# Split halves of the conv outputs' pair sums: adding DMAs or VectorE

## The chip, the cores and the metric

The kernel runs on one core of a Trainium2 chip. The metric is the device time of one launch in microseconds. TensorE (PE) multiplies, VectorE (DVE), ScalarE (ACT) and GpSimd (POOL) work element by element, SyncE (SP) issues DMAs, and GpSimd and ScalarE issue some too. Each engine takes its instructions strictly in the order in which they stand in its own list; an instruction that waits for a semaphore holds up all that stand behind it on that engine.

## The reference

One layer of an encoder on 512 tokens of width 1024, in float32. The attention part (a softmax branch and a stick-breaking branch, gates, an output projection) takes the first half of the run and is not touched here. What matters is the feed-forward part:

```python
def conv_glu(x, w_up, conv_w, conv_b, w_down):
    hid = x @ w_up
    hid = lax.conv_general_dilated(
        hid, conv_w[:, None, :], window_strides=(1,),
        padding=((CONV_WIDTH - 1, 0),),
        dimension_numbers=('NWC', 'WIO', 'NWC'),
        feature_group_count=2 * D_FF) + conv_b
    gate, up = hid[..., :D_FF], hid[..., D_FF:]
    return (jax.nn.silu(gate) * up) @ w_down
```

with `D_FF` = 2816, a convolution of width 3 along the tokens, and x + conv_glu(norm(x)) as the output.

## The kernel before

**Precision.** A float32 product is made of three faster ones: each operand is split into a rounded part (`hi`, a cast on ScalarE) and the rest (`lo`, a subtraction on VectorE), and TensorE adds hi·hi, hi·lo and lo·hi.

**The up-projection** (chunks `up0` to `up21`, 128 gate and 128 up features each). For chunk j TensorE makes the two products against the transposed tokens (`hth`, `htl`), either plainly (`up_body`, 48 matmuls of 512 columns) or, for the twelve chunks in `SEVEN`, by Strassen's scheme in seven products of half the size (`up_seven`, 84 matmuls of 256 columns), whose weight combinations lie in DRAM (`parked`) and are loaded as `wxh`/`wxl` and `w2h`/`w2l`. `conv` then makes the convolution: an activation on ScalarE (L990) and two operations on VectorE (L992, L993), for the gate into `cg` and for the up part into `ub`, a buffer of four slots of 512 tokens, one per chunk. SiLU (L1014) and a product (L1089) make the chunk's output in `ub`. While chunk j is multiplied, the weights of chunk j+1 are split: ScalarE casts `raw_up` into `whi_up` (L242, L271), VectorE subtracts for `wlo_up` (L243, L276), and SP loads the weights after that.

**The pairs.** The down-projection is made by Strassen's scheme too, over pairs of chunks: pair i is chunks 2i and 2i+1, and its seven left operands, each split in two, are kept in `ax` (2048 wide: four operands' hi, then their lo) and `ay` (1536 wide: three operands). They come out of `ub` in two ways: some are its own halves of 256 tokens or their difference in place (`u`, the convolution's output: 768 wide for `ax`, 256 for `ay`), the others are sums that VectorE makes at L1044 into `st` (256 wide for `ax`, 512 for `ay`). `st` is one buffer for all pairs; nothing of the next pair can be written to it until all that read it are done.

`up_fin` calls `pair_sums` behind each odd chunk. For pairs 1 to 8 the split is made by `by_dma`. ScalarE writes the rounded and negated source into the place of the lo half (L1061), a DMA that GpSimd issues adds the source onto it (L1062), and ScalarE casts the source into the place of the hi half (L1063):

```python
A.activation(a[:, n + o:n + sl.stop], src, AF.Copy, scale=-1.0)
G.dma_start(a[:, n + o:n + sl.stop].bitcast(F32), src, accum_op=ALU.add)
A.copy(a[:, sl], src)
```

This is done four times in a pair, for `ay<-st`, `ax<-st`, `ay<-ub` and `ax<-ub`. The other pairs (0, 9 and 10) use `halves`: a cast on ScalarE (L1052) and a subtraction on VectorE (L1053).

**Keeping them.** For pairs 0 to 6 GpSimd then writes `ay` to DRAM (`ayd`, L1095), since there are two buffers for it; SP writes `ax` of pairs 0 and 1 to DRAM (`axd`, L1097). They are loaded again before the down-projection (L1126, L1236).

**The down-projection** (`dn`, L1269) multiplies all pairs' operands with the down weights, in two passes.

**The order.** The kernel's text gives the instructions, and a scheduler with its own estimate of times sets the order on each engine; a change in one place so moves others by a few positions. GpSimd's DMAs need room in SBUF for their descriptors, which is set when the program is made (`dynamic_dma_scratch_size`).

Of the kernel before, what the change touches and what calls it, by code (L numbers as in the profile page):

```python
# [8 lines left out]
F32 = mybir.dt.float32  # L9
# [6 lines left out]
P = 128  # L16
# [58 lines left out]
def block_kernel(ctx: ExitStack, tc: tile.TileContext, x, xt, params, g2, rbx, wts, wd0, wd1, out):  # L75
    nc = tc.nc
    V, A, G, PE, SP = nc.vector, nc.scalar, nc.gpsimd, nc.tensor, nc.sync
# [4 lines left out]
    sm = ctx.enter_context(tc.tile_pool(name="sm", bufs=1))  # L82
# [5 lines left out]
    def apool(name):  # L88
        return ap_ctx.enter_context(tc.tile_pool(name=name, bufs=1))
# [2 lines left out]
        apool(n) for n in ("pv", "pst", "pqn", "ppt", "pwk", "po")]  # L92
    pool_c = apool("pc")
    pool_pk = apool("ppk")
    par = sm.tile([P, 280], F32, tag="par", name="par")
    A.dma_start(par[:, 0:8], params[:, 0:8])
    A.preload_act_table_set("exp_and_others")
    WARM = 9
# [190 lines left out]
    def run_chunk(key, body, pieces=4):  # L289

        sp = split_gen(pos[key] + 1, pieces)
        for _ in body(*splits.pop(key)):
            next(sp, None)
            yield
        for _ in sp:
            pass
# [17 lines left out]
    axd = dram.tile([2, P, 2048], F32, tag="axd", name="axd")  # L314
# [527 lines left out]
    for s in range(len(steps)):  # L842
# [8 lines left out]
        br, h, t, e = pend.pop(0)  # L851
# [131 lines left out]
    pairs = {}  # L983
# [4 lines left out]
    def conv(ps, tile_idx, c):  # L988
        cw = lambda j: par[:, C_CW + 2 * NF * j + tile_idx:C_CW + 2 * NF * j + tile_idx + 1]
        tap = A.activation(c, ps, AF.Identity, scale=cw(2), bias=par[:, C_CB + tile_idx:C_CB + tile_idx + 1])  # L990
        late["tap"] = (tap,)
        V.scalar_tensor_tensor(c[:, 1:], ps[:, 0:S - 1], cw(1), c[:, 1:], op0=ALU.mult, op1=ALU.add)  # L992
        V.scalar_tensor_tensor(c[:, 2:], ps[:, 0:S - 2], cw(0), c[:, 2:], op0=ALU.mult, op1=ALU.add)  # L993
# [17 lines left out]
    def gate(j, pg):  # L1011
        g = fp.tile([P, S], F32, tag="cg", name=f"cg{j}", bufs=1)
        conv(pg, j, g)
        A.activation(g, g, AF.Silu)  # L1014
        return g

    def pair_sums(i):

        u0, u1 = ub[:, 2 * i % 4, :], ub[:, 2 * i % 4 + 1, :]
        u = ub[:, 2 * i % 4:2 * i % 4 + 2, :].rearrange("p a b -> p (a b)")  # L1020
        lo_, hi_ = slice(0, 256), slice(256, 512)
        t = {}
        if i < 8:
            ax = fp.tile([P, 2048], F32R, tag="ax", name=f"ax{i}", bufs=6)
            ay = fp.tile([P, 1536], F32R, tag="ay", name=f"ay{i}", bufs=2)
        elif i == 8:

            ax = fp.tile([P, 2048], F32R, tag="w2h", name=f"ax{i}")
            ay = fp.tile([P, 1536], F32R, tag="ay", name=f"ay{i}", bufs=2)
        else:  # L1030

            ax = late["hp"].tile([P, 2048], F32R, tag=f"ax{i}", name=f"ax{i}")
            ay = late["hp"].tile([P, 1536], F32R, tag=f"ay{i}", name=f"ay{i}")
        pairs[i] = (ax, ay)

        def sums(ops=slice(0, 4)):
            if not t:
                t["st"] = fp.tile([P, 768], F32, tag="st", name=f"st{i}", bufs=1)
                t["s42"] = t["st"][:, 256:768]
                if i == 9:  # L1040

                    t["s42"] = fp.tile([P, S], F32, tag="cg", name="s42_9", bufs=1)
            s1, s4, s2 = t["st"][:, 0:256], t["s42"][:, 0:256], t["s42"][:, 256:512]
            return [V.tensor_tensor(o, x, y, op=op) for o, x, y, op in (  # L1044
                (s1, u0[:, hi_], u1[:, hi_], ALU.add), (u0[:, hi_], u0[:, lo_], u0[:, hi_], ALU.subtract),
                (s2, s1, u0[:, lo_], ALU.subtract), (s4, u1[:, lo_], s2, ALU.subtract))[ops]]

        def halves(a, parts):
            ins, n = [], a.shape[-1] // 2
            for o, src in parts:  # L1050
                sl = slice(o, o + src.shape[-1])
                A.copy(a[:, sl], src)  # L1052
                ins.append(V.tensor_tensor(a[:, n + o:n + sl.stop], src, a[:, sl].bitcast(F32), op=ALU.subtract))  # L1053
            return ins

        def by_dma():

            for a, o, src in ((ay, 256, t["s42"]), (ax, 768, t["st"][:, 0:256]), (ay, 0, u[:, 768:1024]),
                              (ax, 0, u[:, 0:768])):
                n, sl = a.shape[-1] // 2, slice(o, o + src.shape[-1])  # L1060
                A.activation(a[:, n + o:n + sl.stop], src, AF.Copy, scale=-1.0)  # L1061
                G.dma_start(a[:, n + o:n + sl.stop].bitcast(F32), src, accum_op=ALU.add)  # L1062
                A.copy(a[:, sl], src)  # L1063
        if 0 < i < 9:
            return sums, by_dma
        ax_parts = lambda: ((0, u[:, 0:768]), (768, t["st"][:, 0:256]))
        ay_parts = lambda: ((0, u[:, 768:1024]), (256, t["s42"]))
        if i == 0:
            return sums, lambda: halves(ax, ax_parts()), lambda: halves(ay, ay_parts())
        return (lambda: sums(slice(0, 2)), lambda: sums(slice(2, 4)), lambda: halves(ax, ax_parts()[:1]),  # L1070
                lambda: halves(ax, ax_parts()[1:]), lambda: halves(ay, ay_parts()))
# [12 lines left out]
    def up_fin(j, pg, pu, g=None):  # L1084
        if g is None:
            g = gate(j, pg)
        u = ub[:, j % 4, :]
        conv(pu, NF + j, u)
        late["fin"] = (V.tensor_tensor(u, g, u, op=ALU.mult),)  # L1089
        if j % 2 == 1 and j // 2 < 9:  # L1090
            steps = pair_sums(j // 2)
            for step in steps:
                step()
            if j // 2 < 7:
                G.dma_start(ayd[j // 2], pairs[j // 2][1].bitcast(F32))  # L1095
            if j // 2 < 2:
                SP.dma_start(axd[j // 2], pairs[j // 2][0].bitcast(F32))  # L1097

    def up_body(j):
        def body(hi, lo):  # L1100
            pg, pu = BANK(f"pg{j}", j - 1), BANK(f"pu{j}", j - 1)
            yield from up_mm(pg, hi, lo, 0, 0, S)
            g = gate(j, pg)
            if j in (2, 3):
                next(late["ts"])
            held = [] if j + 1 in SEVEN else None
            yield from up_mm(pu, hi, lo, P, 0, S, held)

            def end():
                for mm in held or ():  # L1110
                    mm()
                up_fin(j, pg, pu, g)
            if held:
                late["end"] = end
            else:
                end()
            if j in (2, 3):
                next(late["ts"])
        return body

    def fetch(i):

        tag = {0: "wxh", 1: "wxl", 6: "ax"}.get(i, "ts")
        n, bufs = {"wxh": (1600, 1), "wxl": (1600, 1), "ts": (2048, 4), "ax": (2048, 6)}[tag]
        ay = fp.tile([P, n], F32R, tag=tag, name=f"ay{i}", bufs=bufs)[:, 0:1536]
        G.dma_start(ay, ayd[i])  # L1126
        pairs[i] = (pairs[i][0], ay)
# [80 lines left out]
    halves = []  # L1208

    def up_first(j):  # L1210
        def body(hi, lo):
            pg, pu = BANK(f"pg{j}", 0), BANK(f"pu{j}", 0)
            halves.append((hi, lo, pg, pu))
            yield from up_mm(pg, hi, lo, 0, 0, 256)
            yield from up_mm(pu, hi, lo, P, 0, 256)
            if j == 1:
                n = 0
                for i, (h, l, g, u) in enumerate(halves):
                    for o, ps in ((0, g), (P, u)):
                        for _ in up_mm(ps, h, l, o, 256, S):  # L1220
                            n += 1
                            if n == 1 or 4 <= n < 8:
                                next(late["ts"])
                            yield
                    up_fin(i, g, u)
        return body

    late["ts"] = token_sums()
    for j in range(NF):
        body = up_first(j) if j < 2 else up_seven(j) if j in SEVEN else up_body(j)  # L1230
        for _ in run_chunk(f"up{j}", body, pieces=4 if j < 2 else 2):
            pass
        if j in (SECOND[-1] + 1, SEVEN[-1] + 1):
            i = int(j == SEVEN[-1] + 1)
            ax = fp.tile([P, 2048], F32R, tag=("w2l", "ts")[i], name=f"ax{i}b", bufs=(1, 4)[i])
            SP.dma_start(ax.bitcast(F32), axd[i])  # L1236
            pairs[i] = (ax, pairs[i][1])
            for k in range(5 * i):
                fetch(k)
# [112 lines left out]
    def steps0():  # L1352
        yield
        for i in (9, 10):
            ss[i] = pair_sums(i)
            yield from late_pair(ss[i][:4])
            fetch(i - 4)
# [78 lines left out]
```

## Time and profile before

| | |
|---|---|
| time, median of 3 runs | 748.84 us (746.74 to 749.02) |
| the profiled execution | 752.24 us, its span 750.5 us |
| granted TensorE clock, mean over the span | 0.986 |
| busy: PE / DVE / ACT / POOL | 720.6 / 587.7 / 432.7 / 86.0 us |
| the chain that ended last | PE 79%, DMA 6%, issue 6%, ACT 4%, DVE 4% |
| DMA packets | 154.97 MB, mean 206 GB/s |

Busy times of TensorE are modelled, so 96% of the span is no sign that it runs at its peak. In the tables of waits a row reads: engine, tile and line that waited, then who let it go, the total in microseconds, how often, and the longest. "Issue" is time in which the profile shows nothing that was waited for. Up-projection and the pairs' sums run from about 400 to 650 us, the down-projection from there to the end.

### The profile page before, as it was taken

To read this page: it belongs to the slowest core of one execution; us is meant where nothing else is said; L and a number is where in the kernel's file an instruction comes from. 1 tells how busy PE (TensorE), PEld (TensorE's weight loads), DVE (VectorE), ACT (ScalarE), POOL (GpSimd) and SP (SyncE) were. 2 spreads that over 40 slices of the span, in tenths; PEclk is the share of its full clock that TensorE was granted. 3 is DMA by queue.
4 is the path that set the end of the run, shared out by engine and by line. 5 is a ranking of instruction groups with operands and counts; after the bars stand their busy time and mean duration, and the time that the engine had idled before them with its cause. 6 is when DMAs were issued, how large, how long until landed. Compare 5 with 4: busy or idle time off the path is not lost.

```text
span 750.5 us, 11266 instructions
## 1 busy us (share of the span) xinstructions
PE 720.6 (96%) x4091; PEld 630.7 (84%) x4091; DVE 587.7 (78%) x1049; ACT 432.7 (58%) x803; POOL 86.0 (11%) x123
## 2 busy tenths in 40 slices
PE   9999999999999999999999998986998979999997
PEld 7889998888988888888898898885988869788886
DVE  6678779778999998694667985475848849899687
ACT  7486567577767675342365675455747745544541
POOL 2501300001111121000030011111111121000000
PEclk9999999999999999999999999998998989999999
DMA  9713336352563655769579589875766859765463
GB/s 320 273 58 97 100 106 216 127 196 113 169 221 143 190 203 206 253 228 339 222 280 295 211 261 310 241 219 160 232 169 183 253 141 339 269 211 196 169 224 112
DMA packets 51863, 154.97 MB, mean 206 GB/s; under 512 B 5600, under 2 KB 12384, under 8 KB 44000
## 3 DMA queue, kind: packets, MB, share of 16 engines
q1 hardware_dynamic: 44256, 133.67, 50.7%
q0 software_dynamic: 7264, 20.45, 10.6%
q8 instruction: 32, 0.52, 0.3%
q14 instruction: 23, 0.19, 0.1%
q10 hardware_dynamic: 288, 0.14, 0.1%
HBM read 116.49 MB, written 30.41 MB: 196 GB/s over the span
## 4 chain that ended last, share of the span: by engine, by line
PE 79%; DMA 6%; issue 6%; ACT 4%; DVE 4%; POOL 0%; DVEq 0%; SPq 0%; ACTq 0%; POOLq 0%
PE P L1269 13%; PE p L1171 8%; DMA ay<-st 4%; PE vA L433 3%; PE uA L433 3%; PE gB L300 2%; PE qkB L302 2%; PE gB L301 2%; PE qkB L300 2%; PE gB L302 2%; PE qkB L301 2%; PE wo L300 2%; PE wo L302 2%; PE wo L301 2%; PE pg L300 2%
## 5 line engine op out<-in xcount | busy, mean ns | idle before, releaser
L165 ACT CAST whi_dn<-raw_dn 128x1024 fp32r<-128x1024 f32 x33 | 34.4, 1050 | 26.2 <-DMA raw_dn<-in_wd 13.5
L1269 PE MATMUL P<-whi_dn,ax 128*128 128x512 f32 x144 | 44.7, 390 | 0.0
L161 DVE TENSOR_TENSOR wlo_dn<-raw_dn,whi_dn 128x1024 fp32r<-128x1024 f32 x33 | 40.1, 1223 | 3.6 <-ACT whi_dn L165 3.6
L300 PE MATMUL pg<-hth,whi_up 128*128 128x512 f32 (+1 forms) x96 | 34.9, 364 | 7.2 <-ACT whi_up L271 7.2
L1269 PE MATMUL P<-whi_dn,ay 128*128 128x512 f32 x132 | 40.8, 389 | 0.0
L744 POOL TENSOR_SCALAR_AFFINE_SELECT bB<-bB 128x128 f32<-128x128 f32 x32 | 21.9, 688 | 143.9 <-DVE bB L743 135.2
L1171 PE MATMUL p<-ts,whi_up 128*128 128x256 f32 x192 | 37.0, 288 | 0.0
L1044 DVE TENSOR_TENSOR st<-ub 128x256 f32<-128x256 f32 x11 | 4.6, 421 | 40.1 <-DMA ay<-st 31.5
L1171 PE MATMUL p<-hth,whi_up 128*128 128x256 f32 x96 | 28.2, 294 | 8.0 <-ACT whi_up L242 8.0
L302 PE MATMUL pg<-hth,wlo_up 128*128 128x512 f32 (+1 forms) x96 | 34.7, 361 | 1.2 <-DVE wlo_up L276 1.2
L301 PE MATMUL pg<-htl,whi_up 128*128 128x512 f32 (+1 forms) x96 | 34.7, 362 | 0.0
L207 DVE TENSOR_TENSOR pkr<-pkr 128x512 f32<-128x512 f32 x40 | 27.4, 685 | 8.7 <-DMA pkr<-in_wts 4.3
L300 PE MATMUL pu<-hth,whi_up 128*128 128x512 f32 (+1 forms) x90 | 31.8, 354 | 0.2 <-DVE hg L1197 0.2
L1269 PEld LDWEIGHTS P<-whi_dn,ax 128*128 128x128 f32 x144 | 27.0, 188 | 5.9 <-ACT whi_dn L165 0.3
L301 PE MATMUL pu<-htl,whi_up 128*128 128x512 f32 (+1 forms) x90 | 31.8, 353 | 0.0
L302 PE MATMUL pu<-hth,wlo_up 128*128 128x512 f32 (+1 forms) x90 | 31.5, 350 | 0.0
L1171 PEld LDWEIGHTS p<-ts,whi_up 128*128 128x128 f32 x192 | 31.2, 199 | 0.1
L1171 PE MATMUL p<-hth,wlo_up 128*128 128x256 f32 x96 | 28.1, 293 | 2.7 <-DVE wlo_up L243 2.7
L1171 PE MATMUL p<-ts,wlo_up 128*128 128x256 f32 x96 | 27.8, 289 | 2.6 <-DVE wlo_up L243 2.6
L243 DVE TENSOR_TENSOR wlo_up<-raw_up,whi_up 128x1024 fp32r<-128x1024 f32 x24 | 28.8, 1217 | 0.6 <-ACT whi_up L242 0.6
L1269 PEld LDWEIGHTS P<-whi_dn,ay 128*128 128x128 f32 x132 | 24.8, 188 | 5.1
L1269 PE MATMUL P<-wlo_dn,ax 128*128 128x512 f32 x72 | 28.1, 391 | 0.9 <-DVE wlo_dn L161 0.9
(350 smaller groups left out, 2566.9 us busy)
## 6 DMA issues: line engine op xcount, KB each, us to landing
parked<-pkr SPq DMA_DIRECT2D x45, 256.0 KB, 3.0
raw_dn<-in_wd SPq DMA_DIRECT2D x11, 1024.0 KB, 5.4
pkr<-in_wts SPq DMA_DIRECT2D x10, 1024.0 KB, 6.9
raw_up<-in_wts SPq DMA_DIRECT2D x10, 1024.0 KB, 6.6
raw_up<-in_wts SPq DMA_DIRECT2D x12, 512.0 KB, 6.1
raw_dn<-in_wd SPq DMA_DIRECT2D x11, 512.0 KB, 3.4
wxl_up<-parked SPq DMA_DIRECT2D x21, 256.0 KB, 5.9
ayd<-ay POOLq DMA_DIRECT2D x7, 768.0 KB, 3.9
```

The source lines that it names most:

```text
L161: chain("halves", V.tensor_tensor(o, x, y, op=op))
L165: chain("casts", A.copy(hi[:, sl], src))
L207: V.tensor_tensor(b[o], b[x], b[y], op=op)
L243: V.tensor_tensor(l[:, sl], src[:, sl], h[:, sl].bitcast(F32), op=ALU.subtract)
L300: ins = PE.matmul(ps, sh, mh, start=first, stop=False)
L301: PE.matmul(ps, sh, ml, start=False, stop=False)
L302: PE.matmul(ps, sl, mh, start=False, stop=last)
L433: PE.matmul(pss[t], st[:, 4 * half + k, t * P:(t + 1) * P], mv[:, k, :], start=half == 0 and k == 0 and j == 0, stop=half == 1 and k == 3 ...
L744: G.affine_select(b[:, n - P:n], b[:, n - P:n], pattern=[[-1, P]], compare_op=ALU.is_gt, fill=0.0, base=0, channel_multiplier=1)
L1044: return [V.tensor_tensor(o, x, y, op=op) for o, x, y, op in ((s1, u0[:, hi_], u1[:, hi_], ALU.add), (u0[:, hi_], u0[:, lo_], u0[:, hi_], ...
L1171: PE.matmul(ps, st, mv[:, k, :], start=first and k == 0 and n == 0, stop=last and k == 3 and n == 2, skip_group_check=True)
L1269: chain("products", PE.matmul(dst, st, mv, start=first and n == 0, stop=last and n == 2, skip_group_check=True))
```

## The change

Four things. The two parts of a pair that come out of `st` are split by `halves`, a cast on ScalarE and a subtraction on VectorE; the two that come out of `ub` stay with the adding DMAs. The descriptor room is 1024 bytes a partition for 512, and the tile of parameters is 192 wide for 280. The writes of `ax` to DRAM are put behind chunks 6 and 9, for 1 and 3. Line numbers move a little: L1061 to L1063 before are L1065 to L1067 in the change, L1089 is L1091, L1095 is L1097, and the write of `axd` goes from L1097 to L1234.

```diff
-    par = sm.tile([P, 280], F32, tag="par", name="par")
+    par = sm.tile([P, 192], F32, tag="par", name="par")
...
+        ax_parts = lambda: ((0, u[:, 0:768]), (768, t["st"][:, 0:256]))
+        ay_parts = lambda: ((0, u[:, 768:1024]), (256, t["s42"]))
+
         def by_dma():
 
-            for a, o, src in ((ay, 256, t["s42"]), (ax, 768, t["st"][:, 0:256]), (ay, 0, u[:, 768:1024]),
-                              (ax, 0, u[:, 0:768])):
+            halves(ax, ax_parts()[1:])
+            halves(ay, ay_parts()[1:])
+            for a, o, src in ((ay, 0, u[:, 768:1024]), (ax, 0, u[:, 0:768])):
                 n, sl = a.shape[-1] // 2, slice(o, o + src.shape[-1])
                 A.activation(a[:, n + o:n + sl.stop], src, AF.Copy, scale=-1.0)
                 G.dma_start(a[:, n + o:n + sl.stop].bitcast(F32), src, accum_op=ALU.add)
                 A.copy(a[:, sl], src)
...
-            if j // 2 < 2:
-                SP.dma_start(axd[j // 2], pairs[j // 2][0].bitcast(F32))
...
+        if j in (6, 9):
+            SP.dma_start(axd[j // 9], pairs[j // 9][0].bitcast(F32))
...
-    nc = bacc.Bacc("TRN2", target_bir_lowering=False, num_devices=1, dynamic_dma_scratch_size=512)
+    nc = bacc.Bacc("TRN2", target_bir_lowering=False, num_devices=1, dynamic_dma_scratch_size=1024)
```

GpSimd's list around pair 4, before (its own four adds, the write of its `ay`, the first add of pair 5):

```order
L1062 DMA ay_5294<-ub 128x256
L1062 DMA ax_5293<-st_5295 128x256
L1062 DMA ax_5293<-ub 128x768
L1062 DMA ay_5294<-st_5295 128x512
L1095 DMA ayd<-ay_5294 128x1536
L1062 DMA ay_5551<-ub 128x256
```

and in the change:

```order
L1066 DMA ay_5288<-ub 128x256
L1066 DMA ax_5287<-ub 128x768
L1097 DMA ayd<-ay_5288 128x1536
L1066 DMA ay_5543<-ub 128x256
L1066 DMA ax_5542<-ub 128x768
```

The adds of `st` are gone, the rest keeps its order.

VectorE's list at the sums of the same pair, before:

```order
L1044 TENSOR_TENSOR st_5295<-ub 128x256
L1197 TENSOR_TENSOR hg_5282<-p_10_5278,hu_5283 128x256
L1044 TENSOR_TENSOR ub<-ub 128x256
L1044 TENSOR_TENSOR st_5295<-st_5295,ub 128x256
L1044 TENSOR_TENSOR st_5295<-ub,st_5295 128x256
L1201 TENSOR_TENSOR hu_5283<-p_10_5279,hu_5283 128x256
L992 SCALAR_TENSOR_TENSOR cg_5403<-hg_5282,par,cg_5403 128x511
L1202 TENSOR_TENSOR hu_5283<-hu_5283,pc_5281 128x256
L993 SCALAR_TENSOR_TENSOR cg_5403<-hg_5282,par,cg_5403 128x510
L276 TENSOR_TENSOR wlo_up_5447<-raw_up_5243,whi_up_5446 128x1024 x2
L243 TENSOR_TENSOR wxl_up_5470<-wxl_up_5470,wxh_up_5469 128x1024
```

and in the change (`p` are the chunk's products in PSUM, `hg` and `hu` what is put together of them):

```order
L1044 TENSOR_TENSOR st_5289<-ub 128x256
L1197 TENSOR_TENSOR hg_5276<-p_10_5272,hu_5277 128x256
L1044 TENSOR_TENSOR ub<-ub 128x256
L1044 TENSOR_TENSOR st_5289<-st_5289,ub 128x256
L1053 TENSOR_TENSOR ax_5287<-st_5289,ax_5287 128x256
L1044 TENSOR_TENSOR st_5289<-ub,st_5289 128x256
L1201 TENSOR_TENSOR hu_5277<-p_10_5273,hu_5277 128x256
L992 SCALAR_TENSOR_TENSOR cg_5395<-hg_5276,par,cg_5395 128x511
L1202 TENSOR_TENSOR hu_5277<-hu_5277,pc_5275 128x256
L993 SCALAR_TENSOR_TENSOR cg_5395<-hg_5276,par,cg_5395 128x510
L276 TENSOR_TENSOR wlo_up_5439<-raw_up_5236,whi_up_5438 128x1024 x2
L1053 TENSOR_TENSOR ay_5288<-st_5289,ay_5288 128x512
```

The `ax` half stands between the third and the fourth sum, the `ay` half behind the next weights' subtractions.

SP's list at the write of `ax` of pair 1, before:

```order
L143 DMA raw_up_4762<-in_wts 128x1024
L1097 DMA axd<-ax_4593 128x2048
L230 DMA w2h_up_4904<-parked 128x512
L230 DMA w2l_up_4905<-parked 128x512
L230 DMA w2h_up_4904<-parked 128x512
```

and in the change:

```order
L230 DMA w2l_up_4899<-parked 128x512
L230 DMA w2h_up_4898<-parked 128x512
L230 DMA w2l_up_4899<-parked 128x512
L1234 DMA axd<-ax_4592 128x2048
L148 DMA raw_up_4896<-in_wts 128x2048
```

The write stands behind the six loads of `w2h` and `w2l` now, ahead of the next chunk's weights. Pair 0's write keeps its place in SP's list.

More of the change, by code (lines that the diff above doesn't have):

```diff
@@ L1065, in pair_sums @@
             return sums, by_dma
-        ax_parts = lambda: ((0, u[:, 0:768]), (768, t["st"][:, 0:256]))
-        ay_parts = lambda: ((0, u[:, 768:1024]), (256, t["s42"]))
         if i == 0:
```

## The prediction

> **What bounds the kernel now.** I read the waits of TensorE first, since the page has it busy for 96% of the span. Columns: who waited for whom, microseconds in total, times, longest.
>
> ```profile
> PE p L1171 <- ACT whi_up L242: 8.0, 2, 4.7
> PE pg L300 <- ACT whi_up L271: 7.2, 1, 7.2
> PE p L1171 <- DVE wlo_up L243: 5.3, 4, 2.1
> PE pg L302 <- DVE wlo_up L276: 1.2, 1, 1.2
> PE p L1171 <- DMA w2h_up<-parked: 1.2, 1, 1.2
> ```
>
> These five are 22.9 us, and all of them stand in the up-projection, between 436 and 618 us. They look like waits for ScalarE's casts, but the chain that ended last shows what those casts waited for. This is its piece before the longest of them (start, duration, step):
>
> ```profile
> 497.10 0.86 POOL ax L1062
> 497.96 3.73 issue
> 501.69 8.28 DMA ay<-st
> 510.09 0.43 DVE st L1044
> 510.54 0.35 ACT ax L1061
> 511.24 0.64 issue
> 512.03 0.58 issue
> 512.61 0.74 ACT ax L1063
> 513.35 1.03 ACT whi_up L271
> 514.43 0.79 PE pg L300
> ```
>
> GpSimd can issue the add of `ay<-st` only 3.7 us after its previous one; the add takes 8.3 us to land; only then may VectorE write the single buffer `st` for the next pair; ScalarE's first operation of that pair waits for it, the cast of the next weights stands behind that operation, and TensorE behind the cast. VectorE's own waits give the size of it over all pairs:
>
> ```profile
> DVE st L1044 <- DMA ay<-st: 31.5, 5, 8.4
> DVE st L1044 <- issue: 8.6, 1, 8.6
> DVE hg L1197 <- PE p L1171: 6.3, 3, 3.8
> DVE wxl_up L243 <- ACT wxh_up L242: 2.0, 3, 1.1
> DVE wlo_up L243 <- ACT whi_up L242: 0.6, 2, 0.4
> ```
>
> The first two are one wait: 40.1 us, at six of the eight pairs. Why the adds are late is seen in the list of DMA issues (count, size, microseconds to landing). First the list for the one microsecond from 497 on alone, then the rows of the whole run, which are medians:
>
> ```profile
> ax<-ub POOLq DMA_DIRECT2D x1, 384.0 KB, 4.3
> ```
>
> ```profile
> ayd<-ay POOLq DMA_DIRECT2D x7, 768.0 KB, 3.9
> ...
> ax<-ub POOLq DMA_DIRECT2D x8, 384.0 KB, 4.1
> ...
> ay<-st POOLq DMA_DIRECT2D x8, 256.0 KB, 6.9
> ...
> ay<-ub POOLq DMA_DIRECT2D x8, 128.0 KB, 5.1
> ax<-st POOLq DMA_DIRECT2D x8, 128.0 KB, 4.4
> ```
>
> The add of 497.10 landed at 501.4, and the next was issued at 501.69: an add is not issued before its predecessor has landed, so the four of a pair stand one behind another, 4.1 + 6.9 + 5.1 + 4.4 = 20.5 us by the medians, with some 0.3 us between. One row for the whole stretch (length, then busy time of PE, PE's loads, DVE, ACT, POOL, the granted clock, DMA share, GB/s) says how long a pair is:
>
> ```profile
> 436.00:618.00 182.00, 158.83 (x1062) 145.63 (x1061) 123.10 (x199) 110.24 (x191) 30.14 (x37) 0.95 0.74 215
> ```
>
> Eight pairs in 182 us are 22.8 us each. GpSimd's queue is as full as the pair is long, and `st` hangs at its end. So the binding chain here is GpSimd's queue, by way of VectorE, not TensorE's work.
>
> The stalls cost a second time. After the three longest, the granted clock is halved for some 7 us:
>
> ```profile
> 512.20:519.10 6.90, 4.67 (x11) 3.71 (x12) 5.88 (x8) 6.90 (x11) 0.85 (x1) 0.51 0.51 145
> 566.80:573.80 7.00, 6.29 (x30) 6.29 (x30) 6.56 (x8) 7.00 (x10) 1.73 (x2) 0.51 0.47 119
> 614.60:621.60 7.00, 5.19 (x23) 4.90 (x24) 6.66 (x8) 7.00 (x10) 1.72 (x2) 0.51 0.67 151
> ```
>
> TensorE worked 4.67 + 6.29 + 5.19 = 16.2 us in them, at half speed: 8 us lost. What can be won is 22.9 + 8 = 30.9 us; TensorE alone would need 182 - 30.9 = 151.1 us for the stretch. (The Trainium skill, "TensorE: Matmul & The Clock Gate", Part 1, lets the clock fall to half after an idle window of about 3.4 us. By that rule nothing of the 8 us stays if what is left of the stalls is short, and a stall that stays above it brings its share back; the trace agrees, since the stalls of 1.2 and 2.1 us were followed by no such dip.)
>
> **The change, part by part.**
>
> *Two of four adds a pair go.* GpSimd loses `ax<-st` (4.4 us) and `ay<-st` (6.9 us); its adds of a pair shrink from 20.5 to 9.2 us, and with the write of `ayd` to at most 13.1, against a pair of 151.1 / 8 = 18.9 us when TensorE does not stall. `st` is then read by ScalarE and VectorE alone. VectorE's wait of 40.1 us falls away, because what now frees `st` is an instruction that precedes the next write on VectorE itself. What still reads `ub` by DMA is overwritten two pairs later, two times 18.9 us behind, against 9.2 us of landings: covered.
>
> *VectorE makes the two halves, ScalarE loses its two negated copies.* Both kinds of operation stand in the trace: ScalarE's at the eight pairs of the change, VectorE's at the pairs that it makes already (count; shortest, median and longest in ns; first and last start; shapes):
>
> ```profile
> L1061 ACT ACTIVATE ax<-st x8: 406/418/420, 438.8 to 610.7; 128x256 fp32r<-128x256 f32 x8
> L1061 ACT ACTIVATE ay<-st x8: 614/627/635, 442.4 to 613.0; 128x512 fp32r<-128x512 f32 x8
> L1053 DVE TENSOR_TENSOR ax<-st,ax x3: 413/417/419, 425.8 to 690.2; 128x256 fp32r<-128x256 f32 x3
> L1053 DVE TENSOR_TENSOR ay<-st,ay x2: 681/683/685, 431.5 to 712.4; 128x512 fp32r<-128x512 f32 x2
> ```
>
> VectorE gains 8 x (0.417 + 0.683) = 8.8 us; ScalarE loses 8 x (0.418 + 0.627) = 8.4 us. ScalarE is busy 110 of 182 us, so its relief is worth nothing by itself beyond shorter queues ahead of the weight casts. VectorE's 8.8 us are a real load on an engine that is nearly full once the stretch is short: 123.1 + 8.8 = 131.9 us of work, plus the waits that are not for `st`, 182 - 123.1 - 40.1 = 18.8 us, makes 150.7 us. TensorE needs 151.1. The two are level.
>
> On top come new waits: each of the 16 halves needs ScalarE's cast first. The trace shows no such wait in this stretch. Below it is zero, since the order places the `ay` half a few operations behind its source; above, the longest wait of VectorE for a ScalarE operation here is 1.9 us (row below). The nearest rows are VectorE's other subtractions behind a cast: 0.6 / 2 = 0.3 us each for `wlo_up`, 2.0 / 3 = 0.67 for `wxl_up`. I take their middle, 0.5 us: 16 x 0.5 = 8 us, and VectorE's chain becomes 158.7 us. Some of the 18.8 us will fall away with it, such as the 6.3 us in which VectorE waited for TensorE; I leave that as the reserve for what the new order of the instructions loses in other places.
>
> ```profile
> DVE cg L992 <- ACT cg L990: 2.6, 2, 1.9
> ```
>
> *Descriptor room of 1024 for 512.* A part of why adds wait for each other may be that room; with twice as much the two adds left may overlap. Without it they take 9.2 us of 18.9, with it less: in both cases covered by TensorE's work, so I cost it at nothing. If it did nothing at all the forecast would stand.
>
> *The write of `axd`, one load group later.* On SP the write of pair 1 stood ahead of the loads of `w2h` and `w2l`, and waited:
>
> ```profile
> SPq L1097 <- DMA ax<-ub: 10.3, 1, 10.3
> ```
>
> Queued behind it were six loads; TensorE's 1.2 us for `w2h_up` is theirs. Moved behind them, it costs SP an issue, and the next weight load (`L148`) stands behind it instead, with a chunk of time ahead of its use. The 1.2 us are in the 22.9 already. Nothing else of SP's order moves.
>
> *The order of TensorE, VectorE and ScalarE* is made again, and the rows differ at many places by a few positions. I see no place where work of another stage moves; I give it no term of its own.
>
> **The sum.** The stretch falls from 182 to the longer of 151.1 (TensorE) and 158.7 (VectorE): a gain of 23.3 us. The parts before 436 and after 618 us keep their length: the last step but a few of the chain is TensorE's own work from 652 us on, which these buffers don't touch (start, duration, step):
>
> ```profile
> 652.01 94.16 PE P L1269 x413
> ```
>
> The profiled execution took 752.24 us (span 750.5), 3.4 above the median of the runs shown; 752.2 - 23.3 = 728.9 for it, and 748.8 - 23.3 = 725.5 for the median, which is the forecast.
>
> **The rivals.**
>
> *VectorE becomes the bound.* With a wait w for each half, its chain is 150.7 + 16w. For this speaks the level sum, and that the order puts the `ax` half directly behind the sums, one cast away; against it, the 0.3 and 0.67 us. At w = 1.3 us the chain is 171.5, the gain 10.5 us: 738 us.
>
> *Slower.* The casts of `st` stand in ScalarE's queue behind activations of the convolution and copies that wait for TensorE's products; if a half waits there as VectorE once waited for the DMA, nothing is won and the 8.8 us are added. That decides from 150.7 + 16w = 182, so w = 2.0 us; at 2.5 us the chain is 190.7, and the kernel takes 757.5 us. Against it: no wait of VectorE for ScalarE in this stretch is over 1.9 us.
>
> *No difference.* The adds that are left stay in the way: `ub`'s or `ay`'s buffer takes over the wait of `st`. It needs 18.9 us or more for two adds and a write that now take 13.1, one behind another; the transfers would have to grow by 44%. Time: 749.
>
> **How the numbers follow.** Forecast 0.68, VectorE as the bound 0.18, slower 0.08, no difference 0.06. A difference under 0.3% (2.2 us) can't be told from none. The first two are faster: 0.86; same 0.06; slower 0.08. The range: below, w = 0 and TensorE alone, 748.8 - 30.9 = 718, with 1 us for a shorter tail, 717; above, the second case up to w = 1.4, 150.7 + 22.4 = 173.1, a gain of 8.9 us, 740. The likeliest case's own range is 718 to 733 (w = 1).
>
> **What would show it.** Right: no wait of `st` L1044 for a DMA; TensorE's waits in the stretch under 8 us; no half-clock window between 436 and 618; VectorE's busy time there up by 8.8 us and ScalarE's down by 8.4; 16 adds in place of 32. The step on VectorE is wrong if its waits for the new casts exceed 1 us each. The forecast is wrong if TensorE still waits some 20 us in this stretch, whoever is named, or if the stage behind it grows because its weights come too late.

## The result and the profile after

The change takes 725.64 us (median of 4 runs, 725.04 to 725.95) against 748.93 us before (746.74 to 750.88): a ratio of 0.969, 95% interval 0.966 to 0.972. The forecast was 725.5. It is met to 0.02%, but by luck: two of the steps that led to it are wrong by some 8 us each, with opposite signs. The profiled executions are 752.24 us (span 750.5) before and 725.79 us (span 723.6) after.

TensorE's waits after, over the whole span, answer to the five rows of before:

```profile
PE warm L352 <- DVE warm L349: 1.1, 1, 1.1
PE gA L300 <- DVE mixA L622: 0.3, 1, 0.3
```

Both lie in the attention part and stood there before too. None of the 22.9 us is left. VectorE's waits after, between 410 and 660 us:

```profile
DVE hg L1197 <- PE p L1171: 11.4, 7, 3.6
DVE hu L1201 <- PE p L1171: 4.3, 6, 1.0
...
DVE ub L1091 <- ACT cg L1014: 2.8, 4, 1.2
...
DVE wlo_up L243 <- ACT whi_up L242: 1.3, 1, 1.3
...
DVE ay L1053 <- ACT ay L1052: 0.6, 1, 0.6
```

No wait of `st` for a DMA is left, and the 16 new halves waited 0.6 us in all for their casts. Most of VectorE's remaining waits are now for TensorE: the roles are turned round. The chain that ended last says it in one line (share by engine):

```profile
PE 98%; DVE 1%; ACT 0%; issue 0%; DVEq 0%
```

The same stretch of eight pairs, now from 441.4 to 592.1 us (columns as in the prediction's row: length, PE, its loads, VectorE, ScalarE, GpSimd, clock, DMA share, GB/s):

```profile
441.40:592.10 150.70, 150.70 (x1065) 139.96 (x1064) 131.22 (x216) 104.69 (x176) 17.09 (x22) 1.00 0.80 243
```

182 us became 150.7, all of it TensorE's, at full clock; the prediction's bound for TensorE alone was 151.1. VectorE does 131.2 us in it (131.9 predicted). So the stretch is 8 us shorter than the 158.7 forecast, and the whole should have come out near 718. The rest of the span shows why it did not. Three rows of before, cut at the first matmul of the work, at the first of the up-projection behind the last transposes, at the first of the down-projection and at the last:

```profile
5.12:388.79 383.67, 383.38 (x2115) 332.67 (x2115) 315.13 (x651) 236.13 (x498) 45.44 (x62) 1.00 0.54 194
388.79:639.53 250.74, 227.57 (x1509) 208.70 (x1508) 180.91 (x278) 147.33 (x246) 35.69 (x47) 0.96 0.76 232
639.53:745.77 106.24, 105.29 (x462) 86.29 (x461) 89.42 (x116) 47.20 (x59) 1.07 (x2) 1.00 0.55 194
```

and of after, at the same instructions:

```profile
5.12:394.22 389.10, 388.83 (x2115) 334.41 (x2114) 315.65 (x651) 236.22 (x498) 45.55 (x62) 1.00 0.53 192
394.22:613.64 219.42, 219.42 (x1509) 201.99 (x1508) 188.64 (x296) 141.62 (x230) 21.61 (x31) 1.00 0.80 255
613.64:718.97 105.33, 105.33 (x462) 86.44 (x461) 88.76 (x115) 46.68 (x58) 1.05 (x2) 1.00 0.53 186
```

The up-projection gained 31.3 us. But the first part, the attention, which the change does not touch, takes 5.4 us **more**, with the same 2115 matmuls, under 0.3 us of idle time and a clock of 1.00. The matmuls themselves run slower there. One group of them, the value projection, before (durations shortest, median, longest in ns; first and last start):

```profile
L433 PE MATMUL vA<-whi_vA,hth x32: 389/389/478, 27.9 to 52.6; 128*128 128x512 f32 x32
```

and after:

```profile
L433 PE MATMUL vA<-whi_vA,hth x32: 392/397/480, 28.6 to 53.8; 128*128 128x512 f32 x32
```

By the starts of neighbouring matmuls, a product of `hth` or `htl` with `whi` or `wlo` is followed by the next after 227 ns before and 231 to 237 ns after (medians of 512 columns). (The durations in the rows are longer than that since one matmul starts before the last has ended.) Of the products that use neither `hth` nor `htl`, those of `wo` and `yB` keep their 226 to 227 ns.

### The profile page after: what moved, and what is told of

The parts are those of the page before. It is cut to its first block, busy times and chain, and to the rows that moved or that the text cites. A ratio compares the mean times of both kernels' runs of the same rounds, so it can differ in the third digit from the quotient of the medians.

```text
span 723.6 us, 11241 instructions
## 1 busy us (share of the span) xinstructions
PE 718.0 (99%) x4091; PEld 625.9 (86%) x4091; DVE 595.1 (82%) x1065; ACT 426.7 (59%) x787; POOL 72.0 (10%) x107
## 4 chain that ended last, share of the span: by engine, by line
PE 98%; DVE 1%; ACT 0%; issue 0%; DVEq 0%
PE p L1171 16%; PE P L1271 15%; PE vA L433 3%; PE uA L433 3%; PE pg L301 3%; PE pg L302 3%; PE pg L300 3%; PE pu L302 2%; PE pu L301 2%; PE pu L300 2%; PE gB L301 2%; PE gB L300 2%; PE qkB L301 2%; PE qkB L302 2%; PE qkB L300 2%; PE gB L302 2%
## 5 line engine op out<-in xcount | busy, mean ns | idle before, releaser
L1171 PE MATMUL p<-ts,whi_up 128*128 128x256 f32 x192 | 35.3, 278 | 0.0
L1171 PEld LDWEIGHTS p<-ts,whi_up 128*128 128x128 f32 x192 | 29.4, 188 | 0.0
L742 DVE TENSOR_TENSOR_SCAN aB<-aB,reset 128x127 f32<-128x127 f32 (+3 forms) x32 | 25.9, 816 | 3.0 <-ACT aB L737 2.9
L1171 PE MATMUL p<-htl,whi_up 128*128 128x256 f32 x96 | 26.9, 280 | 0.0
```

The source lines that it names most:

```text
L742: V.tensor_tensor_scan(ar, ar, reset[:, S - n:S - 1][:, ::-1], 1.0, op0=ALU.mult, op1=ALU.max)
L1171: PE.matmul(ps, st, mv[:, k, :], start=first and k == 0 and n == 0, stop=last and k == 3 and n == 2, skip_group_check=True)
```

## The experiments

Each kernel was timed beside the kernel before, whose medians were 748.09, 749.04 and 749.16 us in the three sets; ratios are to the median of the same set.

**The room alone.** The kernel before with the larger room (and the narrower tile of parameters, as in the change); all four adds of a pair stay DMAs, and the instructions' order is that of before.

```diff
-    par = sm.tile([P, 280], F32, tag="par", name="par")
+    par = sm.tile([P, 192], F32, tag="par", name="par")
...
-    nc = ... dynamic_dma_scratch_size=512)
+    nc = ... dynamic_dma_scratch_size=1024)
```

> The kernel before with nothing but the descriptor room at 1024 bytes (and the parameters' tile at 192, which makes the place for it); the order of instructions is that of before. If it is the room that keeps the adding DMAs one behind another, an add is now issued before its predecessor has landed, VectorE's wait of 40.1 us for st shrinks to some 10 to 20 us, and TensorE's stalls of 30.9 us by half or more: 728 to 738 us if nothing else changed. If the adds wait for something else, each is still issued 0.3 us after the landing before, the wait for st stays at 40 us, and the time at 749 us. On the side, a theory on the first 390 us, in which the changed kernel was 5.4 us slower with the same instructions: the place of the weights in SBUF moved by 160 bytes against that of hth and htl. By it this kernel too shows projection matmuls of 232 to 235 ns for 227, and 6 to 7 us more on its time (734 to 745, or 756 if the room does nothing); if that slowness belongs to the chip or the run, it shows 227.

Measured: 725.31 us (724.9 to 726.51), ratio 0.969 [0.966, 0.973]: as much as the whole change. Its DMAs that were issued within 446.5 to 449.5 us (count, size, us to landing):

```profile
ax<-ub POOLq DMA_DIRECT2D x1, 384.0 KB, 8.0
ay<-st POOLq DMA_DIRECT2D x1, 256.0 KB, 7.8
```

Before, a pair's adds stood one behind another, each issued 0.3 us after the landing of the last. Here two that take 8.0 and 7.8 us are issued within 3 us (446.87 and 448.39): they overlap. Over the whole run the medians of `ax<-ub` and `ax<-st` rise from 4.1 to 7.2 and from 4.4 to 6.3 us, those of the other two fall a little (`ay<-st` 6.9 to 6.2, `ay<-ub` 5.1 to 4.9). But from the first issue to the last landing the four adds of a pair take 11.0 to 19.4 us, where they took 17.0 to 25.6 before, and of the wait for `st` this is left:

```profile
DVE st L1044 <- DMA ay<-st: 3.9, 1, 3.9
```

40.1 us became 3.9; TensorE waits 0.7 us in the up-projection. So the adds stood in line for want of descriptor room. And this kernel too has the slow products (their median in the value projection's row is 396 ns).

**The halves alone.** The kernel before with the two `st` parts split by VectorE and nothing else.

```diff
...
-            for a, o, src in ((ay, 256, t["s42"]), (ax, 768, t["st"][:, 0:256]), (ay, 0, u[:, 768:1024]),
-                              (ax, 0, u[:, 0:768])):
+            halves(ax, ax_parts()[1:])
+            halves(ay, ay_parts()[1:])
+            for a, o, src in ((ay, 0, u[:, 768:1024]), (ax, 0, u[:, 0:768])):
...
```

> The kernel before with the halves of st on VectorE alone: room of 512, axd written where it was, places in SBUF as before. If taking st off the adds is what counts, VectorE's wait for st is gone, TensorE's stalls in the up-projection fall from 22.9 to under 3 us and the half-clock windows go: 748.9 - 28 to 31 = 718 to 721 us, faster than the changed kernel, since its weights haven't moved against hth. If the room carries part of the gain (the two adds and the write of a pair, one behind another, still make something late), it comes out above 725. With the write of axd where it was, SP's wait for the add's landing and 1 us of TensorE's wait for w2h may stay.

Measured: 716.82 us (716.62 to 717.5), ratio 0.958 [0.954, 0.962]: 8.8 us quicker than the change. The windows at the same instructions:

```profile
4.96:388.22 383.26, 382.81 (x2114) 331.94 (x2114) 315.36 (x651) 236.20 (x498) 46.41 (x62) 1.00 0.54 195
388.22:605.04 216.82, 216.82 (x1509) 201.50 (x1508) 188.22 (x295) 141.54 (x230) 21.83 (x31) 1.00 0.79 256
```

Here the first part keeps its 383 us, and the up-projection is another 2.6 us shorter than after the change. The two adds that are left still stand one behind the other (the next issued 0.31 us after a landing, at 443.04), but TensorE, VectorE and ScalarE never wait for them, only GpSimd for its own next one and SP for a write of `ax` (4.3 us): the step of the prediction that covered them holds.

**The later writes alone.** The kernel before with the two writes of `ax` moved.

```diff
-            if j // 2 < 2:
-                SP.dma_start(axd[j // 2], pairs[j // 2][0].bitcast(F32))
...
+        if j in (6, 9):
+            SP.dma_start(axd[j // 9], pairs[j // 9][0].bitcast(F32))
```

> The kernel before with only the writes of axd moved. If the stalls come from st, only the wait for w2h (1.4 us) goes, and st's next wait may eat it: 747 to 749 us, no difference that can be told. If SP's 10.3 us of waiting were behind more than that, 740 or less.

Measured: 748.65 us, ratio 0.999 [0.997, 1.002]: no difference. Rows of its waits:

```profile
SPq L1232 <- DMA ax<-ub: 10.1, 1, 10.1
```

```profile
DVE st L1044 <- DMA ay<-st: 30.4, 5, 8.4
DVE st L1044 <- issue: 7.9, 1, 7.9
```

```profile
PE p L1169 <- DMA w2l_up<-parked: 0.7, 1, 0.7
PE p L1169 <- DMA w2h_up<-parked: 0.3, 1, 0.3
```

The write waits as long as before, only something else stands behind it; TensorE's two waits for these loads go from 1.2 + 0.2 to 0.3 + 0.7 us.

**The change without the room.** The changed kernel with the room put back to 512 and the parameters to 280 columns: halves and later writes.

```diff
-    par = sm.tile([P, 192], F32, tag="par", name="par")
+    par = sm.tile([P, 280], F32, tag="par", name="par")
...
-    nc = ... dynamic_dma_scratch_size=1024)
+    nc = ... dynamic_dma_scratch_size=512)
```

> The changed kernel with the descriptor room put back to 512 and the params' tile to 280 columns: halves on VectorE and the later writes of `axd`, no more room. Theory: once the halves are on VectorE, room and writes add nothing, and the placement is the one before: 717 us, within 1.5, as the halves alone (716.8) and as the changed kernel with its placement mended (717.5). If the changed kernel needs the room for its 16 adds left: above 719, with a wait of VectorE or ScalarE for a DMA.

Measured: 716.84 us (716.7 to 717.99), ratio 0.958 [0.954, 0.962], the same as the halves alone. With the halves on VectorE the room gains nothing, and what came with it costs 8.8 us.

**Where the tiles lie.** The room (+512 bytes) and the narrower parameters (-352 bytes) move every tile behind them by 160 bytes, while `hth` and `htl` are counted from the other end of SBUF and stay. In the program's allocation, the operands of these products all stood at 224 modulo 256 before; after, `whi` and `wlo` stand at 128, `hth` and `htl` still at 224. Does that slow the products? First the changed kernel moved by 32 bytes more:

```diff
-    par = sm.tile([P, 192], F32, tag="par", name="par")
+    par = sm.tile([P, 200], F32, tag="par", name="par")
```

> The changed kernel with the parameters' tile 200 wide for 192, so that all that lies behind it in SBUF moves by 32 bytes; the order of instructions is the same, nothing else differs. Theory: matmuls whose two operands start at different remainders of 64 bytes (weights at 0, hth and htl at 32) run at 232 to 235 ns for 512 columns, those with the same remainder at 227. By it the projections return to 227 ns, the first 390 us shorten by 5.4 us, the up-projection by 1 to 2, and the time is 718 to 719 us. If the slower pace came from the chip or the run, the time stays at 725.6.

Measured: 723.34 us (722.57 to 723.61). The products stay slow (229 to 236 ns for 512 columns, one group 226); that 64 bytes would do was wrong. Next, a move by 96 bytes, which makes the difference a multiple of 256:

```diff
-    par = sm.tile([P, 192], F32, tag="par", name="par")
+    par = sm.tile([P, 200], F32, tag="par", name="par")
...
-    nhalf = pool_c.tile([P, 8], F32, tag="nhalf", name="nhalf")
+    nhalf = sm.tile([P, 8], F32, tag="nhalf", name="nhalf")
...
-    qg8 = pool_c.tile([P, 1], F32, tag="qg8", name="qg8")
+    qg8 = sm.tile([P, 1], F32, tag="qg8", name="qg8")
```

> The changed kernel with its tiles put 96 bytes further (params' tile of 200 columns; two small constants moved beside it), so that the first address of `hth` less that of `whi` is a multiple of 256 again, as before the change (178432 before, 178272 after, 178240 with 200 columns; 178176 here); same instructions in the same order. Theory placement (the pace of the products of `hth` and `htl` with `whi` and `wlo` hangs on that difference): 227 ns for each of 512 columns, the part before the up-projection back from 394 to 388-389 us, and 717 us, within 1.5, as the halves alone. Rival (the larger descriptor room itself slows these products, whatever the addresses): 229-235 ns and 723-726 us.

Measured: 717.5 us (717.11 to 718.68), ratio 0.957 [0.952, 0.963]; the products are back at 227 ns, and the first part ends at 388.62 us. The same lines in the kernel with the room alone:

> The kernel before with the room of 1024 and the same placement; the sums are still made by four adds a pair. Theory placement, and that either of room and halves takes the whole stall: 717 us, within 2. If the adds, still four a pair, hold something back that the slow products hid in the first run with the room: 719-724. If the room slows the products: 725.

Measured: 717.72 us (717.13 to 718.35), ratio 0.957 [0.953, 0.962]. So room alone, halves alone and both together take 717 to 718 us once the two sides lie as far apart, modulo 256, as before. Then the reverse, the halves alone (716.82 us) with 32 bytes added, not one instruction or DMA changed:

```diff
-    par = sm.tile([P, 280], F32, tag="par", name="par")
+    par = sm.tile([P, 288], F32, tag="par", name="par")
```

> The halves alone with 32 bytes more in the params' tile: no instruction, no order, no DMA changed, only the addresses of all that lies behind (difference of `hth` and `whi` 32 modulo 64, as in the changed kernel). Theory placement: the products go from 227 to 232-235 ns and the time from 716.8 to 723-726 us. Rival (addresses don't matter; the room slowed the products): 716.8 us, within 1.5.

Measured: 725.8 us (725.33 to 725.98). The group of the value projection reads:

```profile
L433 PE MATMUL vA<-whi_vA,hth x32: 389/395/482, 28.4 to 53.5; 128*128 128x512 f32 x32
```

Thirty-two bytes of padding cost 9 us. With 64 and 128 bytes in place of 32 (296 and 312 columns):

> The halves alone with 64 bytes more: `hth` less `whi` is a multiple of 64, not of 128, as in the changed kernel with 200 columns, which took 723.3 us with 229-233 ns. Theory placement: 722-724.5 us. If only the 32 bytes counted (and the 723.3 came from the room): 717 us.

> The halves alone with 128 bytes more in the params' tile: `hth` less `whi` is 128 modulo 256. If the difference has to be a multiple of 128: 227 ns and 716.8 us, within 1.5. If of 256: products of 229-235 ns and 720-726 us.

Measured: 725.52 us (725.14 to 726.34) and 724.32 us (724.06 to 725.07). 128 is not enough either. The first of the two is 1 us above what was expected from the change with 200 columns, which is 64 off to the other side. Last, is it the difference, or the address of `whi` alone, which stood at 224 modulo 256 in each quick kernel so far? Both sides 32 bytes lower:

```diff
-    par = sm.tile([P, 280], F32, tag="par", name="par")
+    par = sm.tile([P, 272], F32, tag="par", name="par")
...
     htl = hp.tile([P, NK, S], F32R, tag="htl", name="htl")
+    hp.tile([P, 8], F32, tag="pad", name="pad")
```

> The halves alone with `whi` and `hth` both 32 bytes lower (272 columns of params, 32 unused bytes behind `htl`): each address is another, the difference is that of before. Theory that the difference sets the pace: 227 ns, 716.8 us, within 1.5. Rival, that the address of `whi` alone does (224 modulo 256 in each quick kernel so far, 192 here): 723-726 us.

Measured: 717.46 us (717.25 to 717.74); the group's row:

```profile
L434 PE MATMUL vA<-whi_vA,hth x32: 388/390/479, 27.5 to 52.2; 128*128 128x512 f32 x32
```

It is the difference. The down-projection shows it again, within one run. The `ax` and `ay` of pairs 9 and 10 take the place of `hth` and `htl` at the end of SBUF, at 224 modulo 256 in each of these kernels; those of the other pairs lie on the side of the weights. So in the change, with `whi_dn` at 128, the 84 products of pairs 9 and 10 should be slow, and in the last kernel too, which has `whi_dn` at 192 and whose padding moves `hth` and `htl` but not these tiles. They are: 234 ns in the change and 232 to 234 in the last kernel, and 227 for all other pairs (medians). The rows of the `ax` of pairs 9 and 10 (30 of their 32 products with `whi_dn`) in the halves alone, the change and the last kernel:

```profile
L1271 PE MATMUL P<-whi_dn,ax x30: 389/389/390, 654.6 to 664.3; 128*128 128x512 f32 x30
```

```profile
L1271 PE MATMUL P<-whi_dn,ax x30: 392/397/401, 663.2 to 673.2; 128*128 128x512 f32 x30
```

```profile
L1272 PE MATMUL P<-whi_dn,ax x30: 395/396/397, 654.7 to 664.7; 128*128 128x512 f32 x30
```

The kernels without the stall so far, by the difference of `hth` and `whi`:

| `hth` less `whi`, modulo 256 | kernels | us |
|---|---|---|
| 0 | halves; change without room; both sides moved; change placed; room placed | 716.82; 716.84; 717.46; 717.50; 717.72 |
| 64 | change, 200 columns | 723.34 |
| 96 | the change; the room alone | 725.64; 725.31 |
| 128 | halves, 312 columns | 724.32 |
| 192 | halves, 296 columns | 725.52 |
| 224 | halves, 288 columns | 725.80 |

**Is VectorE level with TensorE?** The halves alone, with each of the 16 halves made twice, the cast and the subtraction; the second time writes the same values.

```diff
             halves(ax, ax_parts()[1:])
+            halves(ax, ax_parts()[1:])
             halves(ay, ay_parts()[1:])
+            halves(ay, ay_parts()[1:])
```

> The halves alone (716.8 us), with each of VectorE's 16 subtractions made twice (the second writes the same values): 8.8 us more work on VectorE in the up-projection, 140 of some 150 us. My prediction's step, that VectorE's work and its waits (18.8 us) are level with TensorE: 716.8 + 8.8 = 725.6 us. Rival, that these waits are slack which shrinks as the work grows: 716.8 us, within 1.5, and VectorE's idle time in the stretch falls by about 8 us.

Measured: 717.18 us (716.91 to 717.47), 0.4 us more than with each half made once. The window of the up-projection:

```profile
388.37:604.26 215.89, 215.89 (x1510) 200.56 (x1508) 193.06 (x309) 146.88 (x246) 22.43 (x32) 1.00 0.80 258
```

ScalarE's casts were doubled too, which the expectation left out (16 operations, 8 of some 0.40 and 8 of 0.62 us). VectorE's idle time in the window falls from 216.82 - 188.22 = 28.6 to 215.89 - 193.06 = 22.8 us, by 5.8 in place of the 8 expected (the window holds 14 more instructions of VectorE, not 16, and busy time counts what overlaps only once); its longest group of waits, `hg` for TensorE's products, falls from 9.8 to 6.2 us. The waits are slack, and ScalarE has it too.

## Why the prediction came out right, point by point

*What bounds the kernel, and the first price, 22.9 us of waits.* Right, both in place and size: TensorE sat idle 250.74 - 227.57 = 23.2 us in the up-projection before, and not at all after.

*The second price, 8 us of half clock.* Right, in place and size. TensorE's busy time in the whole stage, for the same 1509 matmuls, fell by more, from 227.57 to 216.82 us with the halves alone, 10.8 us. By the starts of the matmuls, the 61 that begin inside the three dips account for 7.5 us of it. Another 1.9 us is a matter of counting: the last matmul ahead of each of the eleven stalls counts as busy to its end (0.29 us in the mean for 256 columns, 0.39 for 512), where in an unbroken row the next takes over after 0.12 or 0.23. The rest, some 1.3 us, is spread thinly and stays open. The granted clock of the stage, 0.96 over 250.74 us, would say 10 us; but it counts the dips whole, 20.9 us in the prediction's three windows, and TensorE worked only 16.2 of them. (What the Trainium skill says of the clock in "TensorE: Matmul & The Clock Gate", Part 1, agrees: with no wait of TensorE there after the change, the clock stays at 1.00.)

*The cause, adds one behind another holding `st`.* The chain was read rightly, and what broke it was either of two edits. But "descriptor room ... I cost it at nothing" is the first failed step. It holds only because the halves had taken the stall already; alone the room takes all of it (from 749.04 to 717.72 us with the operands as far apart, modulo 256, as before). Had the halves not been in the change, the same reasoning would have missed 31 us. I named the room as a part of why adds wait, and did not ask what it would be worth by itself. The prediction priced one add behind another as a property of the queue; it was one of its room.

*VectorE's load.* Work as predicted: 131.2 us against 131.9. The sum 131.9 + 18.8 = 150.7 looked level with TensorE, but added the waits of the old schedule as though they were fixed. The run with doubled halves shows that they shrink when work is added.

*The new waits, 16 x 0.5 = 8 us.* The second failed step, mis-sized by a factor of 13: 0.6 us in all, 0.04 us a half. I took the middle of two rows of another kind, the subtractions behind the casts of weights; the order, which I had, puts six operations between the last sum and the `ay` half, and that was cover enough. That term alone put the forecast at 725.5 in place of 717.9, which is TensorE's bound.

*The parts outside the stretch keep their length.* The third failed step, and the one that evened out the second. The first part grew by 5.4 us, and the products of the up-projection by 2.6 (219.42 against 216.82 us of the same matmuls). With 105.33 against 104.80 in the down-projection, where the products of pairs 9 and 10 are slow, that makes 8.5 us by the profiled executions; between the medians of the change (725.64) and of the change with its tiles placed (717.50) it is 8.1. The diff showed the cause in two lines, one of which I read as descriptor room only, and the other, the tile of parameters, I did not price at all. That the two errors cancel is luck.

*The later writes.* As costed: nothing that can be measured.

*The rivals.* None came. VectorE did not become the bound even with its new work doubled; it did not wait behind ScalarE's queue; the adds left over disturbed nobody. The case that did come, the whole stall gone and 8 us lost in another place, was not on the list.

The signs that the prediction named all came, with two sizes off: the stage's busy time on VectorE rose by 188.64 - 180.91 = 7.7 us, not 8.8, and on ScalarE it fell by 147.33 - 141.62 = 5.7, not 8.4. Busy time counts overlapping instructions once; the durations of ScalarE's instructions there, added up, fell by 8.0 us. They could not have caught the third step: they looked only into the stretch where the change was made.

## What to carry to other kernels

When two edits of a change could each remove the same stall, price each alone as well as both, and don't read the sum as their parts. After a change that adds or shrinks anything in SBUF, compare the untouched stages too, at the same instructions and matmul counts: a stage that grew there with a clock of 1.00 and next to no idle time can be slow because of where its operands lie. Here the best version is the smallest edit, the halves alone: 716.82 us, 8.8 us quicker than the full change.

## What the runs showed of the hardware

**The pace of matmuls depends on how far apart the two operands lie.** With `hth` less `whi` a multiple of 256 bytes a product of 512 columns is followed by the next after 227 ns; with 32 to 128 bytes off, after 229 to 237 ns in every group but one; for 256 columns 113 to 118 becomes 116 to 121 ns, with some groups unchanged. Over this kernel that is 6 to 9 us of 717. Both roles of the operands show it (`hth` loaded as weights in `vA`, streamed in `gA`), and so do other tiles (`ax` and `ay` of pairs 9 and 10 against `whi_dn`). That the difference decides is shown by moving the weights' side alone and both; why it does is not. It is also open why the groups differ: with 200 columns one of them, `pg<-hth,whi_up`, ran at 226 ns.

**Adding DMAs from GpSimd wait for descriptor room.** With 512 bytes the next was issued some 0.3 us after the landing of the last; with 1024 up to three were in flight at once (two of the four slower for it in the median, such as `ax<-ub`, 4.1 to 7.2 us), and a pair's four adds together were quicker. Why three and not two is open. The Trainium skill, "DMA: Bandwidth & Descriptors", "Anatomy of one DMA", gives about 2 us and the bytes at 436 GB/s for a DMA on this path; an estimate by that page is 2.3 us for the 128 KB of `ay<-ub` and 2.9 us for the 384 KB of `ax<-ub`. In the median of a run the traces have 4.2 to 6.2 and 4.1 to 7.4 us for these adds, beside other traffic, so here the page's figure is too low and the rows decide.

**What stays open.** The kernel before spreads by some 10 us between runs (744.97 to 755.14 us over the last two sets), those without the stall by 1 to 2. Dips of the clock that vary from run to run explain a part of it at most: over its 27 runs in the three sets the granted clock (0.981 to 0.992) goes with the time only loosely (correlation -0.43).
